# Two of four sums of weight quarters per head: accumulating DMAs from GpSimd in place of VectorE

## The chip, the cores and the metric

The kernel runs on one core of one Trainium2 chip. The metric is the device time of one execution in microseconds (us). The core has TensorE (PE, matrix products), VectorE (DVE), ScalarE (ACT), GpSimd (POOL) and SyncE (SP, which here only issues DMAs). Each engine works through its own queue in order, and engines wait for each other by semaphores.

## The reference

One decoder block on 512 tokens of width 2048, in float32. The input is normalised, and one matrix projects it to queries, keys, values and gates. Eight heads of 128 (the first group) mix three attentions: over compressed blocks, over selected blocks and over a window. Sixteen heads of 64 (the second group) attend over a short window with sinks. Each group is multiplied by a gate of its own, an output matrix is applied, and the sum with the input is normalised.

```python
h = _rmsnorm(x, norm_g[l])
proj = h @ w_in[l]
(qa, kca, vca, ksa, vsa, kwa, vwa, za, ga, qb, kb, vb, zb) = jnp.split(proj, offsets, axis=-1)
...
o_a = gates[..., 0:1] * o_cmp + gates[..., 1:2] * o_sel + gates[..., 2:3] * o_win
y_a = o_a.reshape(B, S, WIDTH_A) * jax.nn.silu(za)
...
x = x + jnp.concatenate([y_a, y_b], axis=-1) @ w_out[l]
return _rmsnorm(x, final_g)
```

## The kernel before

Every product is made in a split form: an operand is rounded to a high part (ScalarE, a copy into `whi`) and a low part (VectorE, a subtraction into `wlo`), and `mm3` (lines 112 to 115) issues three matmuls, high by high, high by low and low by high. A weight tile of 128x1024 therefore costs one ScalarE and one VectorE operation before TensorE can use it all.

The first group runs in the loop from line 717. Head 0 projects its query and its gate in the plain way. Heads 1 to 7 go through `pair(h)`, which makes the query and the gate of one head together, as one product of a 2 by 2 block matrix with a 2 by 2 block matrix in the manner of Strassen and Winograd: seven products of quarters instead of eight, at the price of sums of quarters. The sums over the input's side were made earlier and lie in tiles (`pu`, parts of `VH`, `VL`, `KH`, `KL`, `xh`, `xl`); the sums over the weight's side are made in `pair`.

`pair` loads four quarters of the head's weights from device memory (`wq`, 512 KB each, SyncE's queue): `x1` is quarter 3, `x2` quarter 0, `x4` quarter 2 and `x3` quarter 1. `unit` splits a quarter into `whi` and `wlo` (lines 616 and 617, three buffers of each), and `prod` runs its 24 matmuls. In the order of the text the products are "22" (split of `x1`), "p" (split of `x2`), "21" (split of `x3`), "12" (split of `x2 + x4`), "w" (split of `x4 + x1`), "u" (split of `x2 + x4 + x1`) and "q" (the last plus `x3`). The sums are made in place by `plus` (line 665), so the sum of line 679 must wait until both operations of the first split of `x2` have read it, and every later split waits for its sum. `plus` also makes the smaller sums between products, on tiles of 256 columns (`d`, `jj`, `zr`, `qv`).

After the products the rotary embedding is applied to the query on VectorE (lines 704 and 705), summed on GpSimd (line 706), and split (`q_split`, line 477 on ScalarE, line 478 on GpSimd). The four quarters share four buffers (`raw0` to `raw3`) that change roles from head to head, so that a quarter of the next head is loaded as soon as the last use of one of this head's is over. `attn_a(h)` follows `pair(h)` in the text.

The text is not the order in which the engines work. A scheduler orders the instructions of each engine from dependences, the text's order and estimated times, so that the products of head h+1 lie among the attention steps of head h. `tc.issue_after(i)` places instructions behind `i` on their engine; in `pair` it places the first sum of quarters behind the last sum of the head before (`last["jj"]`).

Accumulating DMAs exist in the kernel before: in the output projection `summed` (line 1061) loads a quarter and has GpSimd's queue add a second onto it (line 1065).

Of the kernel before, what the change touches and what calls it, by code (L numbers as in the profile page):

```python
# [13 lines left out]
ALU = mybir.AluOpType  # L14
# [20 lines left out]
def hybrid_block(ctx, tc, xT, xtm, w0, w1s, w2s, wz, wq, wkb, wo0, wos, cw1, cw2, cpos, rope, tabs, sinks, gT, fg, out):  # L35
    nc = tc.nc
    pe, act, dve, pool = nc.tensor, nc.scalar, nc.vector, nc.gpsimd
# [32 lines left out]
    last = {}  # L70
# [403 lines left out]
    def q_split(t1):  # L474
        qh = wk.tile([P, S], F32R, name="qh", tag="qh", bufs=1)
        ql = wk.tile([P, S], F32R, name="ql", tag="ql", bufs=1)
        act.activation(qh, t1, AF.Copy)
        pool.tensor_tensor(out=ql, in0=t1, in1=qh.bitcast(F32), op=ALU.subtract)
        return qh, ql
# [36 lines left out]
    def attn_a(h, qh, ql, st):  # L516
# [4 lines left out]
        for pair in range(2):  # L521
# [77 lines left out]
            for w in range(2):  # L599
                pe.matmul(oc[:, P:256], VF[:, pair, w, g * P:g * P + P], pd[:, w * P:w * P + P], start=False, stop=(w == 1 and pair == 1))  # L600
# [36 lines left out]
    def unit(raw):  # L637
        hi, lo = [wp.tile([P, 1024], F32R, name=nm, tag=nm) for nm in ("whi", "wlo")]
        split(hi, lo, raw)
        return hi, lo  # L640

    def prod(bank, u, op, new):
        for m in range(8):
            cs = slice(m * P, m * P + P)
            ah, al = xf[op, m]
            mm3(bank, u[0][:, cs], u[1][:, cs], ah, al, new and m == 0, m == 7, not new)
# [3 lines left out]
    def load_quarter(src, tag, quarter):  # L650
        t = weights(tag)
        last["dma"] = nc.sync.dma_start(t, src[quarter]).ins
        return t

    def pair(h, *early):
        src = wq[h - FIRST]
        early = list(early)
        c1, c2, c4, c3 = tags
        tags[:] = c4, c1, c3, c2

        def load(tag, quarter):
            return early.pop(0) if early else load_quarter(src, tag, quarter)

        def plus(out, a, b, op=ALU.add):
            return dve.tensor_tensor(out=out, in0=a, in1=b, op=op).ins  # L665

        pa, pb = [psp.tile([P, S], F32, name="pj", tag="pj") for e in range(2)]
        qv = wk.tile([P, S], F32, name="t1", tag="t1", bufs=1)
        zr = wk.tile([P, 2, S], F32, name="zr", tag="xr", bufs=1)[:, 0, :]
        d, jj = qv[:, H1], zr[:, H0]  # L670
        x1 = load(c1, 3)
        u0 = unit(x1)
        x2 = load(c2, 0)
        u3 = unit(x2)
        x4 = load(c4, 2)
        with ExitStack() as behind:
            if "jj" in last:
                behind.enter_context(tc.issue_after(last["jj"]))
            plus(x2, x2, x4)
        prod(pb[:, H0], u0, "22", True)  # L680
        act.activation(d, pb[:, H0], AF.Copy, scale=-1.0)
        x3 = load(c3, 1)
        prod(pa[:, H0], u3, "p", True)
        plus(d, d, pa[:, H0])
        u2 = unit(x3)
        prod(pb[:, H0], u2, "21", False)
        act.activation(zr[:, H1], pb[:, H0], AF.Copy)
        plus(jj, d, zr[:, H1])
        u4 = unit(x2)
        plus(x4, x4, x1)  # L690
        plus(x2, x2, x1)
        prod(pa[:, H0], u4, "12", False)
        act.activation(qv[:, H0], pa[:, H0], AF.Copy)
        plus(jj, jj, qv[:, H0], ALU.subtract)
        u1 = unit(x4)
        prod(pa[:, H1], u1, "w", True)
        plus(d, d, pa[:, H1])
        u5 = unit(x2)
        plus(x2, x2, x3)
        prod(pb[:, H1], u5, "u", True)  # L700
        plus(d, d, pb[:, H1])
        t2 = wk.tile([P, S], F32, name="t2", tag="t2", bufs=1)
        for a, b in ((0, 64), (64, 0)):
            dve.tensor_tensor(out=t2[a:a + 64], in0=qv[b:b + 64], in1=sinA[b:b + 64], op=ALU.mult)
        dve.tensor_tensor(out=qv, in0=qv, in1=cosA, op=ALU.mult)
        pool.tensor_tensor(out=qv, in0=qv, in1=t2, op=ALU.add)
        qq = q_split(qv)
        u6 = unit(x2)
        prod(pb[:, H1], u6, "q", False)
        plus(jj, jj, pb[:, H1])  # L710
        last["jj"] = plus(zr, zr, rstdb, ALU.mult)
        st = wk.tile([P, S], F32, name="st", tag="st")
        act.activation(st, zr, AF.Tanh, scale=0.5)
        dve.scalar_tensor_tensor(out=st, in0=st, scalar=1.0, in1=zr, op0=ALU.add, op1=ALU.mult)
        return qq, st

    for h in range(8):
        if h < FIRST:
            qq = q_evac(q0, cosA, sinA)
            st = z_evac(proj(wz[8], 0))  # L720
            lows, highs = slice(0, 4), slice(4, 8)
            first = []
            with tc.issue_after(last["dma"]):
                first.append(load_quarter(wq[0], tags[0], 3))
                forms_back(0, lows)
                forms_back(1, lows)
            for c, quarter in zip(tags[1:], (0, 2, 1)):
                with tc.issue_after(last["dma"]):
                    first.append(load_quarter(wq[0], c, quarter))
            with tc.issue_after(last["dma"]):  # L730
                for f in (2, 3):
                    forms_back(f, lows)
                    forms_back(f, highs)
        else:
            qq, st = pair(h, *first) if h == FIRST else pair(h)
        attn_a(h, *qq, st)
        if h == 3:
            for e in range(2):
                nc.sync.dma_start((KH, KL)[e][0].bitcast(F32), Kd[e])
            for e in range(2):  # L740
                nc.sync.dma_start((VH, VL)[e][:, 0].rearrange("p t w c -> p (t w c)").bitcast(F32), Vd[e])
# [287 lines left out]
    for n in range(1, 4):  # L1029
        xs.append([late(2 * n - 2 + T) for T in range(2)])  # L1030
        src = wos[n - 1]
# [4 lines left out]
        def scratch():  # L1036
            return so.tile([P, 2, 256], F32, name="e", tag="e", bufs=3)
# [60 lines left out]
        if n < 3:  # L1098
# [3 lines left out]
            jj = scratch()  # L1102
# [28 lines left out]
        else:  # L1131
# [41 lines left out]
            product(bat[0], u3, "p", True, (0,))  # L1173
            do(act.activation, e3[:, 0, :], bat[0][:, 0, :], AF.Copy)
            u0.append(pair())
            do(both, u0[1], r22[1])
            mm(bat[1], u3, "p", True, (1,))
# [141 lines left out]
```

## Time and profile before

| | us |
|---|---|
| three runs, median (lowest to highest) | 829.25 (828.73 to 829.38) |
| the profiled execution | 829.19 |
| its span | 827.4 |
| TensorE busy | 811.5 (98%) |
| VectorE busy | 662.1 (80%) |
| ScalarE busy | 485.6 (59%) |
| GpSimd busy | 89.3 (11%) |

The busy figures are of the profiled execution and its span. Line numbers (L665) are those of the kernel. In a row of the trace, "out<-in" names the tiles that an operation writes and reads; a number in brackets at its end is the time for which the engine stood idle before it, and what ended that. TensorE's matmuls overlap one another, so that a matmul's own duration is longer than the distance to the next one.

### The profile page before, as it was taken

What the parts mean: (1) busy time and instruction counts of PE and PEld (TensorE: products, weight loads), DVE (VectorE), ACT (ScalarE), POOL (GpSimd) and SP (SyncE); (2) the same over time, 40 slices, a digit from 0 to 9 for tenths busy, and PEclk for the clock granted to TensorE, in tenths of its full rate; (3) what the DMA queues carried; (4) which work ended last, traced back from release to release, by engine and by line L of the source; (5) the groups of instructions that cost most, each with busy time, mean ns of one, the idle gap of its engine ahead of it and who ended that gap; (6) DMA issues with size and microseconds to landing.
All of it is one profiled execution on the core that took longest, in us unless ns stands there. A gap on an engine that the chain in (4) does not pass through costs nothing.

```text
span 827.4 us, 14161 instructions
## 1 busy us (share of the span) xinstructions
PE 811.5 (98%) x5278; PEld 735.6 (89%) x5278; DVE 662.1 (80%) x1311; ACT 485.6 (59%) x1026; POOL 89.3 (11%) x69
## 2 busy tenths in 40 slices
PE   9999999999999999999999999999999999999996
PEld 7788898999999999999888888888888788999996
DVE  6869786966799898999766688877677798877895
ACT  6734456564676786787665365645444647554555
POOL 3600002011001001101011121011011000110000
PEclk9999999999999999999999999999999999999998
DMA  9665885898330222522733321222222226797845
GB/s 324 194 206 166 281 290 200 265 371 284 103 111 22 99 77 92 166 90 89 251 107 102 99 92 56 74 80 74 77 76 77 77 62 241 235 251 198 244 96 203
DMA packets 52117, 128.30 MB, mean 155 GB/s; under 512 B 4945, under 2 KB 17233, under 8 KB 52049
## 3 DMA queue, kind: packets, MB, share of 16 engines
q1 hardware_dynamic: 50032, 120.59, 43.3%
q0 software_dynamic: 1728, 6.29, 4.3%
q8 instruction: 41, 0.67, 0.3%
q10 hardware_dynamic: 288, 0.52, 0.2%
q14 instruction: 28, 0.22, 0.1%
HBM read 110.31 MB, written 17.07 MB: 154 GB/s over the span
## 4 chain that ended last, share of the span: by engine, by line
PE 84%; DVE 6%; DMA 5%; issue 2%; ACT 2%; SPq 0%; DVEq 0%; ACTq 0%; POOLq 0%
PE pj L115 16%; PE pj L113 15%; PE pj L114 15%; PE bank L115 4%; PE bank L113 4%; PE oa L114 4%; PE oa L113 4%; PE oa L115 3%; PE sp L539 3%; PE bank L114 3%; PE tp L855 2%; DMA rw<-wos 1%; PE tp L577 1%; DMA xr<-xT 1%; DMA raw<-cw 1%
## 5 line engine op out<-in xcount | busy, mean ns | idle before, releaser
L115 PE MATMUL pj<-xh,wlo 128*128 128x512 f32 (+1 forms) x560 | 196.0, 350 | 2.0 <-DVE wlo L617 1.5
L113 PE MATMUL pj<-xh,whi 128*128 128x512 f32 (+1 forms) x560 | 196.2, 350 | 0.8 <-DVE t L665 0.8
L114 PE MATMUL pj<-xl,whi 128*128 128x512 f32 (+1 forms) x560 | 195.4, 349 | 0.0
L90 DVE TENSOR_TENSOR wlo<-raw,whi 128x1024 fp32r<-128x1024 f32 (+2 forms) x102 | 115.3, 1135 | 37.5 <-ACT whi L89 36.6
L89 ACT ACTIVATE whi<-raw 128x1024 fp32r<-128x1024 f32 (+1 forms) x101 | 95.2, 944 | 80.6 <-PE pj L114 24.0
L115 PEld LDWEIGHTS pj<-xh,wlo 128*128 128x128 f32 x560 | 105.3, 188 | 16.3 <-DVE wlo L617 2.2
L113 PEld LDWEIGHTS pj<-xh,whi 128*128 128x128 f32 x560 | 105.4, 188 | 14.2 <-DVE t L665 1.2
L114 PEld LDWEIGHTS pj<-xl,whi 128*128 128x128 f32 x560 | 105.3, 188 | 13.4 <-issue 0.7
L617 DVE TENSOR_TENSOR wlo<-raw,whi 128x1024 fp32r<-128x1024 f32 x49 | 61.6, 1260 | 10.3 <-ACT whi L616 9.9
L616 ACT ACTIVATE whi<-raw 128x1024 fp32r<-128x1024 f32 x49 | 51.7, 1056 | 24.7 <-PE pj L114 12.7
L113 PE MATMUL oa<-whi,yh 128*128 128x256 f32 (+1 forms) x168 | 50.1, 299 | 0.6 <-ACT yh L909 0.6
L114 PE MATMUL oa<-wlo,yh 128*128 128x256 f32 (+1 forms) x168 | 50.4, 300 | 0.2 <-DVE wlo L1147 0.2
L115 PE MATMUL oa<-whi,yl 128*128 128x256 f32 (+1 forms) x168 | 49.7, 299 | 0.0
L834 ACT ACTIVATE ttb<-ttb,mnb 128x256 f32<-128x256 f32 (+1 forms) x64 | 30.1, 471 | 26.0 <-DVE mnb L827 25.5
L509 DVE TENSOR_TENSOR pl<-tp,ph 128x512 fp32r<-128x512 f32 x56 | 37.6, 683 | 6.6 <-ACT ph L508 6.6
L508 ACT ACTIVATE ph<-tp 128x512 fp32r<-128x512 f32 x56 | 32.3, 592 | 17.9 <-PE tp L577 11.2
L114 PE MATMUL bank<-wlo,xh 128*128 128x256 f32 (+1 forms) x128 | 40.2, 316 | 0.0
L115 PE MATMUL bank<-whi,xl 128*128 128x256 f32 (+1 forms) x128 | 39.9, 314 | 0.0
L468 POOL TENSOR_TENSOR t<-t,t 128x512 f32<-128x512 f32 x9 | 19.3, 2147 | 176.4 <-DVE t L120 176.4
L113 PE MATMUL bank<-xh,whi 128*128 128x512 f32 x96 | 37.0, 396 | 1.1 <-ACT whi L89 0.7
L113 PE MATMUL bank<-whi,xh 128*128 128x256 f32 (+1 forms) x128 | 36.7, 318 | 1.3 <-ACT whi L89 1.3
L114 PE MATMUL bank<-xl,whi 128*128 128x512 f32 x96 | 37.0, 391 | 0.0
(356 smaller groups left out, 2202.2 us busy)
## 6 DMA issues: line engine op xcount, KB each, us to landing
raw<-wz SPq DMA_DIRECT2D x36, 512.0 KB, 3.6
raw<-wq SPq DMA_DIRECT2D x28, 512.0 KB, 3.7
raw<-cw SPq DMA_DIRECT2D x16, 512.0 KB, 5.0
raw<-wos SPq DMA_DIRECT2D x12, 512.0 KB, 5.0
rw<-wos SPq DMA_DIRECT2D x10, 512.0 KB, 5.5
xr<-xT SPq DMA_DIRECT2D x16, 256.0 KB, 5.0
raw<-w SPq DMA_DIRECT2D x8, 512.0 KB, 4.2
fd<-ft SPq DMA_DIRECT2D x4, 1024.0 KB, 5.9
```

The costliest lines, as they stand in the source:

```text
L89: last["hi"] = act.activation(hi[:, :width], rw[:, :width], AF.Copy).ins
L90: last["lo"] = dve.tensor_tensor(out=lo[:, :width], in0=rw[:, :width], in1=hi[:, :width].bitcast(F32), op=ALU.subtract).ins
L113: pe.matmul(ps, ah, bh, start=first, stop=False, skip_group_check=go_on)
L114: pe.matmul(ps, ah, bl, start=False, stop=False, skip_group_check=go_on)
L115: recent["mm"] = pe.matmul(ps, al, bh, start=False, stop=last, skip_group_check=go_on).ins
L468: pool.tensor_tensor(out=t1, in0=t1, in1=t2, op=ALU.add)
L508: act.activation(ph, tp, AF.Copy)
L509: dve.tensor_tensor(out=pl, in0=tp, in1=ph.bitcast(F32), op=ALU.subtract)
L539: pe.matmul(sp[:, a:b], qq[:, qs], kk[0][:, ko:ko + b - a], start=pi == 0, stop=pi == 2)
L616: act.activation(hi, src, AF.Copy)
L617: last["lo"] = dve.tensor_tensor(out=lo, in0=src, in1=hi.bitcast(F32), op=ALU.subtract).ins
L834: act.activation(tv, tv, AF.Exp, bias=mn[:, e, v:v + 1], scale=-1.0, accum_out=dn[:, e, v:v + 1])
```

## The change

`x4 + x1` and `x2 + x4`, the first two sums of weight quarters, are no longer made by VectorE. GpSimd's queue issues two DMAs that read quarter 3 and quarter 2 from device memory once more and add them onto the loaded tiles `x4` and `x2`. The other two sums, `+ x1` and `+ x3` onto `x2`, stay on VectorE. The place behind the last sum of the head before goes with the sum that it held. The edit applies to heads 1 to 7.

```diff
         x2 = load(c2, 0)
         u3 = unit(x2)
         x4 = load(c4, 2)
-        with ExitStack() as behind:
-            if "jj" in last:
-                behind.enter_context(tc.issue_after(last["jj"]))
-            plus(x2, x2, x4)
+        pool.dma_start(x4, src[3], accum_op=ALU.add)
+        pool.dma_start(x2, src[2], accum_op=ALU.add)
         prod(pb[:, H0], u0, "22", True)
...
         u4 = unit(x2)
-        plus(x4, x4, x1)
         plus(x2, x2, x1)
         prod(pa[:, H0], u4, "12", False)
```

## The prediction

> **What bounds the kernel now.** I read the page first, then TensorE's waits and the busy times of the stretch in which the changed function runs (195 to 413 us, the seven heads that go through `pair`).
>
> ```profile
> span 827.4 us, 14161 instructions
> ...
> PE 811.5 (98%) x5278; PEld 735.6 (89%) x5278; DVE 662.1 (80%) x1311; ACT 485.6 (59%) x1026; POOL 89.3 (11%) x69
> ```
>
> ```profile
> 195.00:413.00 218.00, 214.53 (x1723) 208.68 (x1722) 192.22 (x412) 155.78 (x379) 20.46 (x14) 1.00 0.37 120
> ```
>
> ```profile
> PE pj L115 <- DVE wlo L617: 1.5, 3, 0.8
> PE pj L113 <- DVE t L665: 0.8, 2, 0.4
> PE op L584 <- DVE pl L509: 0.4, 1, 0.4
> PE pj L115 <- DVE wlo L90: 0.4, 1, 0.4
> PE sp L539 <- DVE mn L545: 0.3, 1, 0.3
> ```
>
> TensorE is the bound: in the stretch it is busy 214.53 of 218 us at a granted clock of 1.00 (the columns are length, PE, weight load, DVE, ACT, POOL, clock, DMA share, GB/s). VectorE is busy 192.22 of 218, 88%, so it is the nearest rival. The third fence is TensorE's own list of waits in that stretch, all of them for VectorE: eight waits, 3.4 us. That is the first thing to hold on to: whatever VectorE gains, TensorE can get back a few microseconds and no more. The profiled execution took 829.19 us, 1.8 more than its span, and stands 0.06 below the median of 829.25.
>
> How the waits come about is in the timeline of TensorE (start, duration, idle before) and of VectorE.
>
> ```profile
> 261.64 0.28 PE L114 MATMUL pj<-xl,whi 128*128 128x256 f32 x1
> 262.08 0.39 PE L115 MATMUL pj<-xh,wlo 128*128 128x256 f32 x1 [0.16 <-DVE wlo L617]
> ...
> 264.55 0.28 PE L114 MATMUL pj<-xl,whi 128*128 128x256 f32 x1
> 264.66 0.28 PE L115 MATMUL pj<-xh,wlo 128*128 128x256 f32 x1
> 265.36 0.39 PE L113 MATMUL pj<-xh,whi 128*128 128x256 f32 x1 [0.42 <-DVE t L665]
> ...
> 295.04 0.49 PE L539 MATMUL sp<-KH,qh 128*128 128x288 f32 x2 [0.28 <-DVE mn L545]
> ...
> 326.61 0.39 PE L115 MATMUL pj<-xh,wlo 128*128 128x256 f32 x1 [0.83 <-DVE wlo L617]
> ```
>
> ```profile
> 258.58 1.22 DVE L665 TENSOR_TENSOR raw<-raw 128x1024 f32<-128x1024 f32 x1
> ...
> 259.81 2.21 DVE L617 TENSOR_TENSOR wlo<-raw,whi 128x1024 fp32r<-128x1024 f32 x1
> ...
> 262.55 1.21 DVE L665 TENSOR_TENSOR raw<-raw 128x1024 f32<-128x1024 f32 x1
> ...
> 263.76 1.21 DVE L617 TENSOR_TENSOR wlo<-raw,whi 128x1024 fp32r<-128x1024 f32 x1
> 264.90 0.41 DVE L665 TENSOR_TENSOR t<-t,pj 128x256 f32<-128x256 f32 x1
> ...
> 290.79 3.58 DVE L665 TENSOR_TENSOR raw<-raw 128x1024 f32<-128x1024 f32 x2
> ...
> 321.97 3.46 DVE L665 TENSOR_TENSOR raw<-raw 128x1024 f32<-128x1024 f32 x2
> 325.35 1.21 DVE L617 TENSOR_TENSOR wlo<-raw,whi 128x1024 fp32r<-128x1024 f32 x1
> ```
>
> Matmuls of 256 columns start 0.11 to 0.12 us apart (264.55, 264.66). A wait costs more than its idle figure: 264.66 to 265.36 is 0.70, so 0.58 lost for 0.42 of idle, 0.16 more; 261.64 to 262.08 loses 0.32 for 0.16, again 0.16 more. The rows of VectorE show what stands before the late operation: the sums of 128x1024 quarters on line 665, once alone and twice as a pair, 3.58 and 3.46 us in a row.
>
> **What goes.** Each of the seven heads makes four such sums, and two of them go.
>
> ```profile
> L665 DVE TENSOR_TENSOR raw<-raw 128x1024 f32<-128x1024 f32 x28 | 36.1, 1290 | 0.2
> ```
>
> Fourteen of 28 at 1.29 us are 18 us off VectorE, but only TensorE's waits count. Four waits have a removed sum ahead of them in VectorE's queue: 262.08 (the sum at 258.58), 265.36 (the one at 262.55), 295.04 (both at 290.79) and 326.61 (both at 321.97). Their idle is 0.16 + 0.42 + 0.28 + 0.83 = 1.69 us, and with 4 x 0.16 for the restarts 2.3 us. In each the cover is 1.2 us or more of removed work against a wait of under 1 us, so I count them as gone. What comes next in VectorE's queue at these places is the split of the same quarter, already waited for by the same matmuls. The other four waits (the third on line 617, the second on line 665, lines 509 and 90) are behind softmax or evacuation steps, and I leave them as they are. The ordering edge to the end of the previous head (`last["jj"]`) goes as well; it has no cost of its own.
>
> **What comes.** Two DMAs per head, issued by GpSimd, each adding 512 KB from device memory onto a quarter. The trace has ten DMAs of that kind and size on one line of the output projection, onto two kinds of tile.
>
> ```profile
> L1065 POOL DMA_DIRECT2D rw<-wos x4: 862/872/888, 722.2 to 760.6; - x4
> ...
> DMA to landing us min/median/max: 5.5/6.8/10.2
> ```
>
> ```profile
> ch<-wos POOLq DMA_DIRECT2D x6, 512.0 KB, 9.6
> ```
>
> ```profile
> 722.21 0.86 POOL L1065 DMA_DIRECT2D rw<-wos  x1 [17.40 <-DVE late L1085]
> ```
>
> ```profile
> 722.31 1.22 DVE L914 TENSOR_TENSOR wlo<-raw,whi 128x1024 fp32r<-128x1024 f32 x1
> ```
>
> GpSimd is held 0.87 us for each, 14 x 0.87 = 12 us beside 20 us of its own in 218: hidden, unless one stands in front of something urgent (a rival below). VectorE is not slowed by the issue: the subtraction at 722.31 beside the issue at 722.21 takes its usual 1.22. The traffic doubles for two of four quarters; at a DMA share of 0.37 that alone costs nothing.
>
> The price that matters is the landing, 5.5 to 10.2 us where a sum took 1.2. The six onto `ch` have a median of 9.6, so the others are near the lower end. I take the median of all, 6.8, because those rows too were taken beside weight loads, and keep both ends. The sum onto `x4` can start when that quarter has landed, long before its product "w", so it costs nothing. The sum onto `x2` must wait until both halves of that quarter's first split have read it, and then product "12" waits for landing, split to high and split to low. So the room is: start of "12", less the end of the first split, less 2.3 for the new split (1.06 on ScalarE, 1.22 on VectorE). Rows for the first head, the second, the third (its "12" is the matmul at 265.36) and the last:
>
> ```profile
> 195.47 1.06 ACT L616 ACTIVATE whi<-raw 128x1024 fp32r<-128x1024 f32 x1 [0.71 <-PE pj L114]
> ```
>
> ```profile
> 196.56 1.22 DVE L617 TENSOR_TENSOR wlo<-raw,whi 128x1024 fp32r<-128x1024 f32 x1 [4.08 <-ACT whi L616]
> ```
>
> ```profile
> 207.91 0.28 PE L113 MATMUL pj<-xh,whi 128*128 128x256 f32 x1
> ```
>
> ```profile
> 222.52 1.22 DVE L617 TENSOR_TENSOR wlo<-raw,whi 128x1024 fp32r<-128x1024 f32 x1
> ```
>
> ```profile
> 235.01 0.28 PE L113 MATMUL pj<-xh,whi 128*128 128x256 f32 x1
> ```
>
> ```profile
> 250.82 1.22 DVE L617 TENSOR_TENSOR wlo<-raw,whi 128x1024 fp32r<-128x1024 f32 x1
> ```
>
> ```profile
> 378.76 3.45 DVE L617 TENSOR_TENSOR wlo<-raw,whi 128x1024 fp32r<-128x1024 f32 x2
> ```
>
> ```profile
> 393.81 0.29 PE L113 MATMUL pj<-xh,whi 128*128 128x256 f32 x1
> ```
>
> Start of "12" is counted as the 25th matmul from the start of "21", which has 24. First head: 207.91 - 197.78 - 2.3 = 7.8 us. Second: 235.01 - 223.74 - 2.3 = 9.0. Third: 265.36 - 252.04 - 2.3 = 11.0. Last: 393.81 - 382.21 - 2.3 = 9.3. For the three between I estimate the mean of the last three figures, 9.8. A landing of 6.8 fits into every one, so the change puts no wait on TensorE; at 10.2 it would.
>
> A rule of the Trainium skill would make this safer still. "DMA: Bandwidth & Descriptors", section "Anatomy of one DMA — SWDGE (gpsimd) path", gives a DMA from GpSimd about 2.0 us plus its bytes over 436 GB/s, so an estimated 3.2 us for 512 KB; by it the sum is the same, and the slow rival below would be out of reach. The trace's 5.5 to 10.2 for the accumulating kind disagrees, and I go by the trace.
>
> **The sum.** 829.2 - 2.3 + 0 = 826.9 us. No more than all eight waits can come back: 3.4 + 8 x 0.16 = 4.7 us, so the floor is 824.5.
>
> **Rivals.** First, *late landings* (slower). Landings come out at the slow end, 10.2, as with a busy DMA system in the first head, whose window shows this share (0.87, the last but one column):
>
> ```profile
> 190.00:200.00 10.00, 10.00 (x52) 8.52 (x51) 5.67 (x8) 3.08 (x4) 2.60 (x2) 1.00 0.87 304
> ```
>
> Then "12" is late by 2.4 in the first head, 1.2 in the second, 0 in the third, 0.9 in the last, and 0.4 in each of three: 5.7 us, and 829.2 - 2.3 + 5.7 = 832.6. It breaks even near 9.5 us of landing and is slower by 0.2% from 9.9. The instruction order is made anew for the changed program, from estimated times; if it places "12" earlier, each microsecond of that counts like one of landing, and a split that waits for a DMA holds the softmax steps queued behind it on ScalarE. Against: half of the ten landings are at or under 6.8, and the DMA share of the whole stretch is 0.37.
>
> Second, *the waits only move* (no change). Every engine's order is new, and the one before, whatever its merits, left 4.7 us of waits; a new one may leave as many elsewhere: 829.2. For it: half of the present waits are not behind a removed sum at all. Against: VectorE has 18 us less to do.
>
> Third, *GpSimd's queue* (no change). GpSimd works in order, and the DMA onto `x2` may be placed ahead of the rotary sum of the running head. In the last head that would hurt:
>
> ```profile
> 379.01 2.12 POOL L706 TENSOR_TENSOR t<-t,t 128x512 f32<-128x512 f32 x1 [26.85 <-DVE t L705]
> ```
>
> The first split ends at 382.21, so the rotary sum would start at 383.1 and not 379.01, 4.1 us late, and the scores of that head with it: at most 829.2 - 2.3 + 4.1 = 831.0, and 829.2 if other matmuls fill half of that. In the second head the split ends before the rotary sum is due, and nothing is lost.
>
> Fourth, *a busy VectorE holds up the issue* (no change): if GpSimd could not issue while VectorE works, an issue would wait for up to the longest operation above, 2.21 us. The landing would be 9.0, 1.2 too late in the first head: 828.1. The issue beside a subtraction at 722 speaks against it. The Trainium skill has such a rule in "SBUF — State Buffer", section "SBUF: two separate sides": descriptors written by GpSimd starve while VectorE runs a mode that takes both ports. The trace does not show it at that place.
>
> **How the numbers follow.** About 0.2% (1.7 us) is what a measurement of this kernel can tell from no change. Forecast: 0.44, faster. Late landings: 0.31, slower. Moved waits 0.15, GpSimd's queue 0.06, held-up issue 0.04: 0.25 within 0.2%. The range reaches from 825.0, which needs nearly the whole of the 4.7, to 833.0, just over the landing of 10.2. The forecast's own range is 825.0 to 827.6, where 0.2% begins.
>
> **What would show it.** Right: 14 sums left on line 665, VectorE about 18 us less busy, no wait of TensorE on a split behind a sum, landings of the new DMAs under 7.8 us in the first head. Wrong: ScalarE's split waiting for a DMA with TensorE waiting behind it; landings near 10; a rotary sum on GpSimd starting later after the last row of `pair`'s VectorE work than now; or a list of TensorE's waits as long as before with other names.

## The result, and the profile after

| | us |
|---|---|
| with the change, median of 6 runs (lowest to highest) | 834.54 (831.95 to 835.82) |
| before, beside it, median of 6 runs (lowest to highest) | 829.32 (828.73 to 831.33) |
| ratio, with its 95% interval | 1.0059 (1.0040 to 1.0078) |
| the profiled execution with the change | 831.95 |

The change makes the kernel slower by 0.6%, about 5 us, where I had forecast 2.3 us less. Two later comparisons of the same kernels gave 1.0052 (1.0034 to 1.0069) and 1.0047 (1.0029 to 1.0064). The profiled execution is the lowest of its six runs, so the profile shows less of the loss than the six runs together: 831.95 against 829.19 in the profile of before.

The page with the change, the span and the busy times:

```profile
span 830.1 us, 14185 instructions
...
PE 813.5 (98%) x5278; PEld 736.5 (89%) x5278; DVE 651.8 (79%) x1297; ACT 483.8 (58%) x1026; POOL 100.4 (12%) x83
```

The stretch of the seven heads, with the same columns as before:

```profile
195.00:413.00 218.00, 213.88 (x1717) 207.70 (x1716) 179.22 (x398) 156.99 (x383) 31.96 (x26) 1.00 0.56 149
```

and the sums that are left to VectorE:

```profile
L665 DVE TENSOR_TENSOR raw<-raw 128x1024 f32<-128x1024 f32 x14 | 17.1, 1218 | 0.1
```

The edit does what it says. Fourteen sums are gone, 19.0 us of that group, and VectorE is busy 179.22 us of the stretch and no longer 192.22 (two other groups grew a little, by some 2 us together; the rest of the difference I have not followed). TensorE, which was to profit, is busy 213.88 of 218 us and no longer 214.53. Its list of waits in the stretch:

```profile
PE pj L113 <- DVE dn L557: 2.2, 3, 1.0
PE sp L539 <- DVE mn L545: 0.6, 1, 0.6
PE pj L113 <- ACT whi L616: 0.3, 1, 0.3
PE tp L577 <- ACT tt L567: 0.3, 1, 0.3
PE pj L113 <- DVE t L665: 0.3, 1, 0.3
```

3.7 us and no longer 3.4, in seven waits and no longer eight. None is behind a removed sum. Of the four that I had counted out, three are gone, and of the scores' wait of 0.28 us some 0.15 is left, which the list leaves out; others stand in their place. What is new is on ScalarE. Its waits in the stretch, of which the first two of one kind of instruction are shown, the split to the high part:

```profile
ACT whi L616 <- PE pj L114: 8.7, 10, 1.8
...
ACT whi L616 <- DMA raw<-wq: 6.2, 4, 2.3
```

Four splits wait 6.2 us for a DMA. The landings of the DMA onto `x2` (line 677) and then of the one onto `x4` (line 676), in the view by line:

```profile
L677 POOL DMA_DIRECT2D raw<-wq x7: 862/880/887, 197.5 to 378.9; - x7
...
  ACT whi L616: 6.2, 4
...
DMA to landing us min/median/max: 5.2/5.4/9.2
```

```profile
DMA to landing us min/median/max: 5.4/6.2/9.7
```

Line 677's DMA is the one waited for; in the same view of line 676 nobody is listed as waiting. And yet the landings are quick: a median of 5.4 us, under the 6.8 that I had taken. The wait is there because the new order brings ScalarE to the split before the data has landed. The timeline shows one place from the issue to TensorE:

```profile
320.60 0.88 POOL L677 DMA_DIRECT2D raw<-wq  x1 [1.49 <-DVE zr L665]
...
326.14 1.06 ACT L616 ACTIVATE whi<-raw 128x1024 fp32r<-128x1024 f32 x1 [2.11 <-DMA raw<-wq]
...
327.24 1.23 DVE L617 TENSOR_TENSOR wlo<-raw,whi 128x1024 fp32r<-128x1024 f32 x1 [2.48 <-ACT whi L616]
...
328.70 0.28 DVE L545 CUSTOM_DVE_ANT_0 tt<-sp,tab 128x128 f32<-128x128 f32 x1
...
329.14 0.49 PE L539 MATMUL sp<-KH,qh 128*128 128x288 f32 x2 [0.62 <-DVE mn L545]
```

GpSimd issues at 320.60. ScalarE is done with what stands ahead of the split at 326.14 - 2.11 = 324.03, so the order leaves the DMA 3.4 us; the data lands after some 5.5. ScalarE stands for 2.11 us, then VectorE, whose next operation is the other half of that split, for 2.48, and behind that half on VectorE are the softmax steps of the running attention (line 545). The scores' matmul at 329.14 waits for those. So TensorE is held up by a softmax step, three queues away from the DMA that is late.

### The profile page after: what moved, and what is told of

It is laid out like the page before. It is cut to its first block, busy times and chain, and to the rows that moved or that the text cites. A ratio compares the mean times of both kernels' runs of the same rounds, so it can differ in the third digit from the quotient of the medians.

```text
span 830.1 us, 14185 instructions
## 1 busy us (share of the span) xinstructions
PE 813.5 (98%) x5278; PEld 736.5 (89%) x5278; DVE 651.8 (79%) x1297; ACT 483.8 (58%) x1026; POOL 100.4 (12%) x83
## 4 chain that ended last, share of the span: by engine, by line
PE 79%; DVE 7%; DMA 6%; ACT 4%; issue 3%; POOL 0%; SPq 0%; DVEq 0%; ACTq 0%; POOLq 0%
PE pj L113 15%; PE pj L114 14%; PE pj L115 14%; PE bank L115 4%; PE bank L113 4%; PE bank L114 4%; PE sp L539 3%; PE oa L114 3%; PE oa L115 2%; PE oa L113 2%; DMA rw<-wos 2%; PE tp L852 1%; DMA xr<-xT 1%; PE tp L577 1%; DMA ch<-wos 1%
## 5 line engine op out<-in xcount | busy, mean ns | idle before, releaser
L468 POOL TENSOR_TENSOR t<-t,t 128x512 f32<-128x512 f32 x9 | 16.4, 1817 | 169.6 <-DVE t L120 169.4
```

Of the source, the lines that this page charges most:

```text
L468: pool.tensor_tensor(out=t1, in0=t1, in1=t2, op=ALU.add)
```

## The experiments

An edit may give every engine a new order of instructions, and how far that happened decides what an experiment can say; it is told with each set.

**First set: the change once more, its halves, and neither sum.** The change itself again:

> The changed kernel once more, for a second profile: the first one was of its fastest run (832.0 of 832.0 to 835.8), while the kernel before keeps within 1 us. Theory A (late landing: in the order that the changed program got, the split of the summed x2 stands so early on ScalarE that it waits for the accumulating DMA, and steps queued behind it reach TensorE late): 832 to 836, ScalarE waits for DMA on line 616 in at least 4 heads, and the waits of TensorE are longer than the first profile's where the landings are longer. Theory B (order alone: the new order of VectorE leaves as many waits elsewhere): 832 to 836 too, but with the same waits of TensorE at the same places as in the first profile, whatever the landings.

834.74 us against 830.0, ratio 1.0052 (1.0034 to 1.0069). It stays slower, and six of ScalarE's splits wait 7.4 us for the DMA.

Only the sum onto `x4` by DMA, issued in the place of line 690, with the sum onto `x2` and its ordering edge left on VectorE:

```diff
-        plus(x4, x4, x1)
+        pool.dma_start(x4, src[3], accum_op=ALU.add)
```

> Only the sum x4 + x1 goes to an accumulating DMA (issued after the sum of x2, which reads x4 first); x2 + x4 stays on VectorE behind the previous head's last sum. Theory A: its landing is not needed before the product w, so 828 to 830, as before. Theory B: a new order, anywhere from 827 to 835.

838.16 us, ratio 1.0097 (1.0071 to 1.0123): above both expected ranges.

Only the sum onto `x2` by DMA, without the edge, and `x4 + x1` left on VectorE:

```diff
-        with ExitStack() as behind:
-            if "jj" in last:
-                behind.enter_context(tc.issue_after(last["jj"]))
-            plus(x2, x2, x4)
+        pool.dma_start(x2, src[2], accum_op=ALU.add)
```

> Only the sum x2 + x4 goes to an accumulating DMA; x4 + x1 stays on VectorE. Theory A: this is the harmful half, 832 to 836, with ScalarE waiting for DMA on line 616 as in the changed kernel. Theory B: a new order, anywhere from 827 to 835, not tied to landings.

838.5 us, ratio 1.0087 (1.0064 to 1.0109): above both again. Each half alone is dearer than both together, so the halves do not add up, and neither can be read as a part of the price: each program was given an order of its own. In both, ScalarE's splits wait for the DMA 1.5 to 1.8 times as long as with the change (first the one onto `x4`, then the one onto `x2`), and a part of the price is TensorE's clock (see the last section):

```profile
ACT whi L616 <- DMA raw<-wq: 11.2, 5, 2.6
```

```profile
ACT whi L616 <- DMA raw<-wq: 11.4, 6, 3.5
```

Neither sum, by no engine:

```diff
-        with ExitStack() as behind:
-            if "jj" in last:
-                behind.enter_context(tc.issue_after(last["jj"]))
-            plus(x2, x2, x4)
...
-        plus(x4, x4, x1)
```

> Both sums are left out, and nothing takes their place (two of the seven products get wrong operands): VectorE's relief without DMAs. Theory A: faster than before by the waits behind the sums, 825 to 828. Theory B: the relief by itself reorders for the worse, 831 to 835.

830.83 us, ratio 1.0006 (0.9992 to 1.0020). This kernel leaves two sums of each head out and pays nothing for them anywhere, and it is no faster. TensorE's waits in the stretch:

```profile
PE op L584 <- DVE pl L509: 1.8, 1, 1.8
PE pj L115 <- DVE wlo L617: 0.8, 2, 0.6
PE sp L539 <- POOL ql L478: 0.5, 1, 0.5
PE pj L113 <- ACT t L677: 0.3, 1, 0.3
```

3.4 us, the sum of before again, in five waits at other matmuls (line numbers are those of each kernel: 677 is here ScalarE's evacuation of product "22"). The time lies between the ranges of the two theories. VectorE's relief together with this order is worth nothing that can be measured.

**Second set: the adding, the place of the DMAs, the place of the split, and the edge.** Both DMAs copy and do not add, so the sums are left out; the queues, the bytes and the waits are those of the change:

```diff
-        pool.dma_start(x4, src[3], accum_op=ALU.add)
-        pool.dma_start(x2, src[2], accum_op=ALU.add)
+        pool.dma_start(x4, src[3])
+        pool.dma_start(x2, src[2])
```

> The changed kernel with its two DMAs copying instead of adding (the sums are left out: the quarters are overwritten). The order of the instructions is the same on every engine as in the changed kernel, row by row; only the landing is shorter (I expect about 4 us from GpSimd's queue, against 5.4 to 6.2) and the traffic on the tile's side halves. Theory A (late landing): ScalarE's waits for DMA on line 616 fall from 6 to 7 us to under 3, and the time from 834.7 to 830 to 832. Theory B (order): 834 to 835.5, with the waits of TensorE at 345, 377 and 408 us as they are.

830.74 us against 832.47, ratio 0.9991 (0.9973 to 1.0010): the whole loss is gone, as theory A has it. Every engine has the same instructions in the same order as with the change, so only the DMAs themselves differ, in what they do, in their duration and in GpSimd's time for the issue (0.57 us and 0.88 in the rows below and above). The view of line 677 in this kernel:

```profile
  ACT whi L616: 1.0, 2
...
DMA to landing us min/median/max: 3.5/3.9/7.4
```

and the timeline at the place shown above:

```profile
321.19 0.57 POOL L677 DMA_DIRECT2D raw<-wq  x1 [1.49 <-DVE zr L665]
...
325.10 1.06 ACT L616 ACTIVATE whi<-raw 128x1024 fp32r<-128x1024 f32 x1 [0.48 <-DMA raw<-wq]
326.19 1.23 DVE L617 TENSOR_TENSOR wlo<-raw,whi 128x1024 fp32r<-128x1024 f32 x1 [0.84 <-ACT whi L616]
...
328.89 0.41 PE L539 MATMUL sp<-KH,qh 128*128 128x288 f32 x2
```

The room is again 3.4 us (321.19 to 325.10 - 0.48 = 324.62). The copy lands in 3.9, so the split starts 0.48 late and not 2.11, and the matmul at 328.89 waits for nothing. A copy nearly fits this order and an addition does not.

The same sums, formed so that the DMA for the earlier product adds quarter 0 onto `x4`, whose first split comes only after the sum, and not quarter 2 onto `x2`; the other DMA adds quarter 2 onto `x1`:

```diff
-        pool.dma_start(x4, src[3], accum_op=ALU.add)
-        pool.dma_start(x2, src[2], accum_op=ALU.add)
+        pool.dma_start(x4, src[0], accum_op=ALU.add)
+        pool.dma_start(x1, src[2], accum_op=ALU.add)
...
-        u4 = unit(x2)
+        u4 = unit(x4)
...
-        u1 = unit(x4)
+        u1 = unit(x1)
```

> The same two sums by DMA, but onto tiles that no near split holds back: quarter 0 is added onto x4 (its sum feeds product 12, and it can start as soon as x4 has landed), quarter 2 onto x1 once its split for product 22 has read it (that sum feeds w, one product later). VectorE keeps two sums as in the changed kernel. Theory A: ScalarE waits less for DMA than in the changed kernel, 828 to 832. Theory B: another order, 828 to 838, and no tie to the waits for DMA.

837.61 us, ratio 1.0073 (1.0046 to 1.0100). Here ScalarE's splits wait for no DMA of `wq` at all, and yet the kernel is no faster than with the change (the intervals of the two ratios overlap). Theory A, 828 to 832, is missed. In TensorE's list other waits stand in the place of that one:

```profile
PE op L584 <- DVE pl L509: 3.9, 2, 2.1
PE pj L113 <- DVE dn L556: 1.1, 2, 0.5
```

So taking the late landing away by another arrangement did not help: the arrangement brought another order.

The split of the summed `x2` held behind ScalarE's evacuation of product "21":

```diff
-        act.activation(zr[:, H1], pb[:, H0], AF.Copy)
+        out21 = act.activation(zr[:, H1], pb[:, H0], AF.Copy).ins
...
-        u4 = unit(x2)
+        with tc.issue_after(out21):
+            u4 = unit(x2)
```

> The changed kernel with both operations of the split for product 12 placed behind ScalarE's evacuation of product 21, so that ScalarE's softmax steps are not queued behind a wait for the DMA. Theory A: ScalarE's waits for DMA nearly vanish, and the time falls to 829 to 833, unless the later split makes TensorE wait for product 12 itself. Theory B: 832 to 838.

841.47 us, ratio 1.0118 (1.0095 to 1.0141), above both expected ranges. No split waits for an adding DMA any more, as theory A had it, but a later place for the split costs more than the wait. TensorE's list (line 691 is here ScalarE's evacuation of product "12"):

```profile
PE sp L539 <- DVE mn L545: 4.0, 9, 1.0
PE pj L113 <- ACT t L691: 3.9, 4, 1.1
```

The kernel before without the ordering edge, all four sums on VectorE:

```diff
-        with ExitStack() as behind:
-            if "jj" in last:
-                behind.enter_context(tc.issue_after(last["jj"]))
-            plus(x2, x2, x4)
+        plus(x2, x2, x4)
```

> The kernel before without the edge that places the first sum of quarters behind the last sum of the previous head; all four sums on VectorE. It is the part of the change that has no DMA. Theory A: at most 2 us from before, 828 to 832. Theory B: a new order by itself, 831 to 836, part of the loss.

844.5 us, ratio 1.0150 (1.0125 to 1.0175): 12 us for one edge, the dearest of all and far above both expected ranges. TensorE waits for smaller sums and for the query, behind the big sums on VectorE:

```profile
PE pj L113 <- DVE zr L665: 4.4, 3, 2.0
PE sp L539 <- ACT qh L477: 2.9, 1, 2.9
PE pj L115 <- DVE wlo L617: 1.7, 3, 0.6
```

**Third set: which of the two landings.** All four kernels were run on one chip, and all have the order of the change on every engine; they differ in which of the DMAs adds (a sum whose DMA copies is left out).

> The changed kernel beside the next three, all four with the same order of instructions on every engine: 833 to 836, as before.

> Both DMAs copy instead of adding (no sums), on the same chip as the changed kernel. If the 4 us between them (834.7 against 830.7, on different chips) are real: 829 to 832 where the changed kernel has 833 to 836.

The DMA onto `x4` copies, the one onto `x2` adds:

```diff
-        pool.dma_start(x4, src[3], accum_op=ALU.add)
+        pool.dma_start(x4, src[3])
```

> Only the DMA onto x4 copies (that sum is left out), the one onto x2 adds. Theory A1 (the landing of x2 alone, which product 12 waits for): as the changed kernel, 833 to 836. Theory A2 (traffic of the accumulating kind, wherever it goes): half way, 831.5 to 833.5.

The DMA onto `x2` copies, the one onto `x4` adds:

```diff
-        pool.dma_start(x2, src[2], accum_op=ALU.add)
+        pool.dma_start(x2, src[2])
```

> Only the DMA onto x2 copies (that sum is left out), the one onto x4 adds. Theory A1: as with both copied, 829 to 832. Theory A2: half way, 831.5 to 833.5.

| `x2`'s DMA | `x4`'s DMA | median us | ratio to before (95%) | ScalarE's splits wait for the DMA, us |
|---|---|---|---|---|
| adds | adds | 832.84 | 1.0047 (1.0029 to 1.0064) | 7.4 |
| adds | copies | 831.81 | 1.0037 (1.0016 to 1.0058) | 10.0 |
| copies | adds | 830.48 | 1.0004 (0.9991 to 1.0017) | 1.5 |
| copies | copies | 829.23 | 0.9988 (0.9972 to 1.0004) | 1.4 |

The slower landing onto `x2` costs 832.84 - 830.48 = 2.4 us, or 831.81 - 829.23 = 2.6. The one onto `x4` comes out at 1.0 and 1.3, but the intervals of the two pairs overlap, so that is not shown. The times alone do not decide between the theories: the second row, 831.81, lies in the range of A2 and below that of A1, and so does the change itself, 832.84; the third lies in that of A1. The last column cannot be compared to a microsecond: in the first row two more waits, of 0.81 and 0.85 us at the splits of the sixth and seventh head, are put down to TensorE, though the DMA had landed 0.08 us before them.

The traces of these kernels can be laid on one another matmul by matmul, which takes out the stages that the change does not touch. The distance from the start of the 1,000th matmul (at 183 to 185 us) to that of the 3,600th (at 565 to 580) encloses all places at which TensorE's orders differ; counted in the trace of one execution each:

| kernel | us |
|---|---|
| before | 382.05 |
| neither sum | 381.53 |
| both copy (two executions) | 381.69, 382.11 |
| `x2` copies, `x4` adds | 381.91 |
| `x4` copies, `x2` adds | 385.50 |
| the change (three executions) | 384.15, 383.80, 385.09 |
| swapped quarters | 387.87 |
| only `x2` by DMA | 389.73 |
| only `x4` by DMA | 391.05 |
| split held | 391.59 |
| no edge | 395.15 |

Here the division is sharper than in the times, and it is that of A1. Wherever `x2`'s DMA adds in this order, the stretch is 1.7 to 3.8 us longer than where it copies; `x4`'s adds nothing. And the order itself, with the sums gone, is within 0.5 us of the one before.

Between the change and the copying kernels the distance grows in steps, at the same matmuls in every pair: 0.2 to 0.6 us at 269.8 (after the split at 263.89, which waited 2.34), 0.6 to 0.9 at 329.1 (the chain shown above) and 0.37 at 345.5; two more of 0.1 to 0.3, at 357 and 388, I have not followed to a DMA. In the two longest executions, both of the third set, another 0.5 us comes between 236 and 243, after the second head's split, which waited 1.9 us there and 1.1 in the other two. The step at 345.5 is the remainder of the one at 329, sixteen microseconds later. First the change, then the copying kernel:

```profile
344.87 0.17 DVE L556 TENSOR_SCALAR dn<-dn 128x6 f32<-128x6 f32 x1 [0.49 <-ACT tt L555]
344.94 0.42 DVE L665 TENSOR_TENSOR t<-t,pj 128x256 f32<-128x256 f32 x1
...
345.51 0.36 PE L113 MATMUL pj<-xh,whi 128*128 128x256 f32 x1 [0.99 <-DVE dn L557]
```

```profile
343.81 0.17 DVE L556 TENSOR_SCALAR dn<-dn 128x6 f32<-128x6 f32 x1 [0.49 <-ACT tt L555]
...
344.80 0.36 PE L113 MATMUL pj<-xh,whi 128*128 128x256 f32 x1 [0.60 <-DVE dn L557]
```

The two executions reach the 1,000th matmul 0.91 us apart, the copying one later, so differences between them are larger by that than they look; but the distance is the same at both places: the split at 326.14 against 325.10 (1.04), VectorE's next step after the exponentials at 344.87 against 343.81 (1.06). Nothing is caught up in between, and the sum (line 665) for the next head's first product stands behind the softmax step. The 0.60 that is left in the copying kernel belongs to the order.

## Why the prediction was wrong

**TensorE's waits as the bound** held. Where both sums are free, the stretch gains at most 0.5 us of 382, and VectorE's 13 us less show nowhere else.

**The gain of 2.3 us** failed. Three of the four waits did go and the fourth is halved, much as predicted, but the step from "these waits go" to "this time comes back" took the rest of the list to stay as it was. With a new order of every engine the list came out at 3.4 us without the sums and 3.7 with the change. This is my second rival, *the waits only move*, and I had given it 0.15. The evidence against it, VectorE's 18 us, was time that by my own first paragraph TensorE could not get back. One reading was wrong besides, without a change to the sum: the matmuls at 262.08 and 326.61 belong to product "21", so the split behind the sum is there that of quarter 1 and not that of the summed quarter.

**The landing**, 6.8 us taken from rows of 5.5 to 10.2, was on the safe side: 5.4 for `x2`, 6.2 for `x4`. From the rule of the Trainium skill ("DMA: Bandwidth & Descriptors", section "Anatomy of one DMA — SWDGE (gpsimd) path") I had an estimate of 3.2 us. The copies landed in 3.5 to 7.4 us with a median of 3.9, the additions in 5.2 to 9.2 with a median of 5.4; so the rule is 0.7 us short for a copy and 2.2 for an addition, and the 1.5 us between the two are what decides here.

**The room** was read to the wrong end, and this is the step that failed most. I had it up to TensorE's product "12", 7.8 to 11 us, and concluded from "a landing of 6.8 fits into every one" that "the change puts no wait on TensorE". Room of that kind was there: by the same formula, from the DMA's issue, the new order leaves 6.5 to 13.2 us in the seven heads, every landing fits, and "12" starts without a wait in all of them. Rows of the third head, where it is shortest:

```profile
258.60 0.88 POOL L677 DMA_DIRECT2D raw<-wq  x1 [1.45 <-DVE wlo L617]
...
263.89 2.01 ACT L616 ACTIVATE whi<-raw 128x1024 fp32r<-128x1024 f32 x2 [2.34 <-DMA raw<-wq]
...
267.35 0.28 PE L113 MATMUL pj<-xh,whi 128*128 128x256 f32 x1
```

Up to "12" it is 267.35 - 258.60 - 2.3 = 6.5 us. But the first to stand for the data is ScalarE, which comes to the split 263.89 - 2.34 - 258.60 = 2.95 us after the issue here and 3.4 at 320.60; in the second to seventh head it is 3 to 5 us. There the additions land in 5.2 to 5.6 us and the copies in 3.5 to 4.4. What is late then is not "12" but the softmax steps behind the split. The first head shows the reverse: the addition took 9.2 us, more than the 7.8 that I had set as the limit there, and nobody waited, since ScalarE came to that split 10 us after the issue.

The order is the same whether the DMA adds or copies, and it fits the copy; that the scheduler's estimate takes the two for alike is my inference from this. I had written down what happened as a clause of the first rival, *late landings*: that a split that waits for a DMA holds ScalarE's softmax steps. But I priced that rival by long landings, 9.5 us and up, and drew its break-even from the room to "12", so its 832.6 us is near the result for another reason than the one I worked out, by luck.

**Nothing for the DMA onto `x4`**: nobody waits for it in the trace, and the matmuls' distances show no price. The 1.0 and 1.3 us between the medians stay open.

**"It has no cost of its own"**, said of the ordering edge, was wrong as a statement about the edge: with the sums on VectorE its loss costs 12 us. With the sum gone nothing is left for it to order, and sums and edge together went without a cost that can be measured.

**GpSimd's queue and the held-up issue** did not show. GpSimd is held 0.86 to 0.89 us for each issue as predicted (1.01 for the first), no wait of TensorE in the stretch is put down to it, and the landings are no longer than at line 1065.

What is not settled is the size. In the matmuls' distances the change costs 1.8 to 3.0 us against before; the three comparisons, by their ratios, 3.9 to 4.9. Ahead of the 1,000th matmul and behind the 3,600th, where TensorE's instructions are the same in all kernels, the executions differ by 2 and 3.6 us among themselves, which may hide the rest or be it.

No version that makes all the sums was faster than the kernel before.

## What to carry to other kernels

Where a scheduler makes the order anew, the room for a slower replacement must not be read from the old trace, nor only up to the product that needs the data: every engine that works in order stands from the moment when its queue comes to that data. Here that was 3 to 5 us behind the issue, and the difference between the copy that fits and the addition that does not decided. To test such a replacement, keep the order and change only its duration (here a copy for an addition), since a change of a half of the edit changes the order too and can cost more than the whole. And an engine with 88% of busy time gave nothing back here when it was relieved: the bounding engine waited 3.4 us in all, and in the new orders it waited about as long elsewhere (2.9 to 3.7).

## What the runs showed of the hardware

**Adding costs a DMA from GpSimd about 1.5 us.** In one and the same order, 512 KB onto `x2` lands in 5.2 to 9.2 us with the addition and in 3.5 to 7.4 without it (medians 5.4 and 3.9).

**Short waits can be followed by half of TensorE's clock.** Where only `x4` is summed by DMA, two waits of 1.02 and 1.53 us lie close together at 290 us, and the next 3.40 us are granted half the clock (three windows of 3.40 us, the clock is the third number from the end):

```profile
289.30:292.70 3.40, 0.85 (x5) 0.42 (x5) 3.40 (x8) 1.34 (x4) 1.33 (x2) 1.00 0.79 133
292.80:296.20 3.40, 3.40 (x16) 3.16 (x16) 2.65 (x11) 3.40 (x10) 0.00 (x0) 0.50 0.38 95
296.30:299.70 3.40, 3.40 (x28) 3.27 (x28) 1.70 (x5) 2.53 (x10) 0.00 (x0) 1.00 0.62 182
```

16 matmuls fit where the next window has 28 (they are in part of other shapes). The Trainium skill ("TensorE: Matmul & The Clock Gate", section "Part 1: The HAM clock gate") puts the fall to half rate after an idle window of about 3.4 us. The length of the slow part agrees, but here TensorE had worked in the 3.40 us ahead of it, for 0.85. The kernel without the edge shows the same at its wait of 2.9 us, for 6.80 us. With the change itself, whose longest wait is 0.99, the clock stays at 1.00 in the stretch. A wait alone does not decide it: with neither sum TensorE waits 1.77 us at 263 and keeps the full clock.

Such stretches are a part of the price of the kernels that got an order of their own: two of 3.40 us with only `x4` by DMA, one with only `x2`, one with the swapped quarters, and 3.40 and 6.80 us without the edge. There matmuls of 256 columns start 0.21 us apart (297.84, 298.05) and not 0.12, so an estimate is that nearly half of such a stretch is lost: some 3 of the 9.0 us by which only `x4` lies above before in the table of distances, and 4 to 5 of the 13.1 without the edge. The kernels with the order of the change have none in the stretch.

**Matmuls can be 4% slower at a granted clock of 1.00.** In some executions the output projection, whose instructions are the same in all kernels, runs at 172 matmuls in 20 us, in others at 178 or 179. Of the kernels of the third set, first the one in which both copy, then the one in which only `x2` copies:

```profile
745.00:765.00 20.00, 20.00 (x172) 20.00 (x171) 15.13 (x17) 7.91 (x8) 1.76 (x2) 1.00 0.67 184
```

```profile
745.00:765.00 20.00, 20.00 (x178) 20.00 (x178) 15.26 (x17) 8.66 (x11) 1.73 (x2) 1.00 0.68 189
```

Three of the fourteen traces have it. From the start of the 4,500th matmul to that of the 5,000th (730 to 787 us before the change) these three take 58.89 us each and the other eleven 56.67. The 2.2 us are nearly the whole effect of a landing, and a reason to compare such kernels stretch by stretch; what brings the slower rate is not shown.
